# An FFN up-projection loop on one core: each product tied behind the one ahead of it on TensorE

## The chip, the core and the metric

The kernel runs on one core of one Trainium2 chip. The core has engines with queues of their own: TensorE (PE, matrix products, with its weight loads shown as PEld), VectorE (DVE), ScalarE (ACT), GpSimd (POOL) and SyncE (SP, which issues most DMAs). The metric is the device time of one execution in microseconds. A profile of one execution is shown beside it.

## The reference, cut to what matters

A trunk of two layers over a stream x of 1024 positions and 1024 channels, float32. Each layer has a mixer (layer 0 recurrent, layer 1 with attention) and then the gated MLP below. The change touches the product `x @ w_up` of that MLP, in both layers.

```python
D_MODEL, SEQ, DEPTH, D_FF, FFN_CONV = 1024, 1024, 2, 2816, 3

def conv_glu_ffn(x, w_up, conv_w, conv_b, w_down):
    h = causal_depthwise_conv(x @ w_up, conv_w, conv_b)
    gate, val = jnp.split(h, 2, axis=-1)
    return (jax.nn.silu(gate) * val) @ w_down
...
        h = h + conv_glu_ffn(rmsnorm(h, ffn_norm[layer]), ffn_up[layer], ffn_conv_w[layer],
                             ffn_conv_b[layer], ffn_down[layer])
```

## The kernel before

**Precision.** Every float32 product is done as three matmuls. An operand a is split into a high part (a cast on ScalarE, `split`, L389) and a low part (the difference on VectorE, L390); the products are high x high, high x low and low x high. A pair of weight buffers is called wh and wl (or wh2x and wl2x, when it comes from a second pool), the pair of a half-size block dh and dl.

**Blocks.** The up-projection makes 22 blocks of 128 gate channels g and 128 value channels v, numbered f. Positions come in two halves of 512. For f from 1 on, g and v of a block are taken together as a 2 x 2 problem (two outputs, two halves of the input channels), and by a scheme of the Strassen kind it takes seven products instead of eight. Their names in the code are "11", "21", "2", "1", "3", "22", "4". Each product is four chunks of 128 input channels times three matmuls, twelve matmuls of 128 x 512 (`prod`, L777). The input side is made ready once per layer (tiles AH, AL, TH, TL), the weight side per block by `prep_a` to `prep_d`: these sum and split the raw weights (wst) on VectorE and ScalarE for the next block.

**PSUM.** In blocks 2 to 21 four products ("11", "2", "3", "4") accumulate into one bank X, one behind the other, and ScalarE copies X out after each of the first three (p1, L1125; u2, L1135; u3, L1150) and after the fourth (v, L1165). "21" writes y_, the first half of a tile YZ of two banks; "1" and then "22" write z_, its second half. VectorE adds y_ and p1 into one half of g (L1131); ScalarE copies z_ after "1" (p5, L1145); VectorE makes the other halves of v (L1157) and g (L1159). There are four buffers of the kind of X and two of YZ.

**The block before.** While block f is multiplied, the tail of block f-1 runs on the other engines: two activations that start the convolution (L793, L794, `ident`), four taps on VectorE (L799), a silu (L807), a product (L813) and sums that are stored for the down-projection (L823 to L844). In the source the tail's pieces stand between the products of block f. The tail of block 0 stands whole before the loop, behind block 1's products (`prev.whole()`).

**Order.** The program is traced line by line, and a planner then places each instruction on its engine's queue by its own estimate of when the operands are there; among those that are ready, the one traced earlier goes first. Each engine works through its queue in that order and waits at an instruction whose semaphores are not there. `tc.issue_after(ins)` puts what is traced inside it behind `ins` on the same engine, in the planner's order alone, with no semaphore. In the kernel before, the loop holds one such tie for products:

```python
            with tc.issue_after(p4.ins) if f == 2 else nullcontext():
                prod(X, w["a"], 0, "11")
```

p4 is the last matmul of block 1's "4". All other products of the loop are placed as the planner sees fit.

Of the kernel before, what the change touches and what calls it, by code (L numbers as in the profile page):

```python
# [175 lines left out]
def trunk(ctx: ExitStack, tc: tile.TileContext, x, mix0_norm, mix0_w_in, lru_conv_w, lru_conv_b,  # L176
# [74 lines left out]
    def t4(name):  # L251
        return tmp.tile([P, T], F32, tag="t4", bufs=4, name=name)

    def t2(name):
        return tmp.tile([P, H], F32, tag="t2", bufs=4, name=name)

    def pbig(name):
        return psum["big"].tile([P, T], F32, tag="big", name=name)
# [16 lines left out]
    def psml(name):  # L275
        return sml.tile([P, H], F32, tag="sml", name=name)
# [159 lines left out]
    last = {}  # L436

    class Start:
# [24 lines left out]
        def do(self, eng, ins):  # L463

            def trace(fn):
                with ExitStack() as behind:
                    if eng in last:
                        behind.enter_context(tc.issue_after(last[eng].ins))
                    last[eng] = fn()
                return last[eng]  # L470

            return trace(ins)
# [237 lines left out]
    def ffn(ly, norms):  # L710
# [27 lines left out]
        def prep_a(f):  # L738
            w = ws[f] = {"g": W.take(f"{ly}g{f}"), "v": W.take(f"{ly}v{f}"), "a": W.pair()}
            split(*w["a"], w["g"])  # L740

        def prep_s(f, n):
            w = ws[f]
            g, v = w["g"], w["v"]
            if n == 0:
                s1 = w["s1"] = (t2(f"s1{ly}{f}") if w2[0] is None else
                                w2[0].tile([P, H], F32, tag="s1", bufs=2, name=f"s1{ly}{f}")
                                ).rearrange("p (k m) -> p k m", k=4)
                dve.tensor_tensor(s1, v[:, 0:4], v[:, 4:8], op=ALU.add)
                dve.tensor_tensor(v[:, 0:4], g[:, 0:4], v[:, 0:4], op=ALU.subtract)  # L750
            else:
                dve.tensor_tensor(g[:, 0:4], w["s1"], g[:, 0:4], op=ALU.subtract)
                dve.tensor_tensor(g[:, 4:8], g[:, 4:8], g[:, 0:4], op=ALU.subtract)

        def prep_b(f):
            w = ws[f]
            w["b"] = W.pair()
            low = split(*w["b"], w["g"])[1]
            W.done()
            return low  # L760

        def prep_c(f):
            w = ws[f]
            w["c"] = W.pair()
            split(*w["c"], w["v"])
            W.done()

        def prep_d(f):
            w = ws[f]
            w["d"] = [fd.tile([P, 4, P], F32R, tag=t, name=f"{t}{ly}{f}") for t in ("dh", "dl")]  # L770
            split(*w["d"], w["s1"])

        def prod(ps, x, k0, y, first=True):
            (xh, xl), (yh, yl) = x, Y[y]
            for k in range(4):
                for i, (a, b) in enumerate(((xh, yh), (xh, yl), (xl, yh))):
                    last = pe.matmul(ps, a[:, k0 + k], b[:, k],  # L777
                                     start=(first and k == 0 and i == 0),
                                     stop=(k == 3 and i == 2), skip_group_check=True)
            return last  # L780
# [135 lines left out]
        def bring(g, y, j):  # L916

            ks = slice(2 * j, 2 * j + 2)
            r = t4(f"br{ly}{g}{y}{j}").rearrange("p (k t) -> p k t", k=2)
            nc.sync.dma_start(r, hids[ly][g][:, OPS[y], ks])  # L920
            return lambda: split(*(t[:, ks] for t in B[y]), r)

        def brings(g, ys):
            return [lambda y=y, j=j: bring(g, y, j) for y in ys for j in range(2)]
# [137 lines left out]
        def prep(n):  # L1062

            q, i = steps_[n]
            q.preps[i]()
            nxt = quads.index(q) + 1
            if nxt < len(quads):
                if q.form == "A":
                    loads = {1: (0,), 2: (1,)}.get(i, ())
                else:  # L1070
                    loads = {0: (0,), 2: (1,)}.get(i, ())
                for j in loads:
                    quads[nxt].load(j)
# [3 lines left out]
        w = ws[1]  # L1077
        X, R, y_, z_ = (psml(f"{n}{ly}1") for n in ("X", "R", "y", "z"))
# [24 lines left out]
        p4 = prod(X, w["c"], 4, "4", False)  # L1103
# [5 lines left out]
        prev.ident()  # L1109

        first_ = brings(0, ("11", "2", "3", "4"))
        for f in range(2, NF):
            if f == NF - 1:
                W.more = None
                quads[0].load(0)
                came = [b() for b in first_[:2]]
            w, nxt = ws.pop(f), f + 1 if f + 1 < NF else None
            X = psml(f"X{ly}{f}")
            YZ = pbig(f"YZ{ly}{f}")
            y_, z_ = YZ[:, HALF[0]], YZ[:, HALF[1]]  # L1120
            g, v = t4(f"g{ly}{f}"), t4(f"v{ly}{f}")
            with tc.issue_after(p4.ins) if f == 2 else nullcontext():
                prod(X, w["a"], 0, "11")
            p1 = t2(f"p1{ly}{f}")
            act.copy(p1, X)  # L1125
            if nxt:
                prep_a(nxt)
            prev.conv_g()
            prod(y_, w["a"], 4, "21")
            prev.silu()  # L1130
            dve.tensor_tensor(g[:, HALF[0]], y_, p1, op=ALU.add)  # L1131
            prev.conv_v(1)
            prod(X, w["b"], 0, "2", False)
            u2 = t2(f"u2{ly}{f}")
            u2_ = act.copy(u2, X)  # L1135
            if not nxt:
                with tc.issue_after(u2_.ins):
                    for do in came:
                        do()
                came = [b() for b in first_[2:4]]  # L1140
            prev.conv_v(0)
            prev.end()
            prod(z_, w["d"], 0, "1")
            p5 = t2(f"p5{ly}{f}")
            act.copy(p5, z_)  # L1145
            if nxt:
                prep_s(nxt, 0)
            prod(X, w["c"], 0, "3", False)
            u3 = t2(f"u3{ly}{f}")
            u3_ = act.copy(u3, X)  # L1150
            if nxt:
                prep_s(nxt, 1)
                prep_d(nxt)
            else:
                quads[0].load(1)
            prev.sums()
            dve.tensor_tensor(v[:, HALF[1]], p5, u3, op=ALU.add)  # L1157
            prod(z_, w["b"], 4, "22", False)
            dve.tensor_tensor(g[:, HALF[1]], z_, u2, op=ALU.add)  # L1159
            if nxt:  # L1160
                prep_b(nxt)
            else:
                prep(0)
            prod(X, w["c"], 4, "4", False)
            act.copy(v[:, HALF[0]], X)  # L1165
            if nxt:
                prep_c(nxt)
            prev = Tail(f, g, v)
            prev.ident()
# [181 lines left out]
        for f0, n in PLAIN[ly]:  # L1351
            a = slots[f0 - PLAIN[ly][0][0]:][:n]
# [583 lines left out]
    for s_ in order[:-1]:  # L1936
        if s_ == "mix0":
            norm = mix0(norm)
        elif s_ == "mix1":
            norm = mix1(norm)  # L1940
        else:
            norm = ffn(int(s_[-1]), norm)
# [35 lines left out]
```

## Time and profile before

| what | value |
|---|---|
| runs | 2123.05, 2125.86 and 4249.69 us; median 2125.86 |
| profiled execution | 2124.15 us, span 2122.4 us, granted TensorE clock 0.999 |
| TensorE busy | 2089.6 us, 98% of the span, 9580 matmuls |
| VectorE, ScalarE busy | 1603.5 us (76%), 1063.7 us (50%) |
| up-projection loop, f = 2 to 21 | layer 0 from 383.5 to 771.9 us, layer 1 from 1497.8 to 1886.8 us of the span |

Times in the rows are microseconds from the span's start. A row of the timeline gives the start, the duration, engine, line of the kernel, operation, what is written and read by the names of the program, shape and count, and in brackets how long the engine sat idle before and what ended that. A row of the stage table gives a window, its length, and per engine the busy time in it with the number of instructions that touch it; then the granted clock of TensorE as a share, the busy share of the DMA engines and GB/s. Matmuls overlap, and their ends in the record are modelled, so distances between starts are used for TensorE, not durations.

### The profile page before, as it was taken

To read this page: it belongs to the slowest core of one execution; us is meant where nothing else is said; L and a number is where in the kernel's file an instruction comes from. 1 tells how busy PE (TensorE), PEld (TensorE's weight loads), DVE (VectorE), ACT (ScalarE), POOL (GpSimd) and SP (SyncE) were. 2 spreads that over 40 slices of the span, in tenths; PEclk is the share of its full clock that TensorE was granted. 3 is DMA by queue.
4 is the path that set the end of the run, shared out by engine and by line. 5 is a ranking of instruction groups with operands and counts; after the bars stand their busy time and mean duration, and the time that the engine had idled before them with its cause. 6 is when DMAs were issued, how large, how long until landed. Compare 5 with 4: busy or idle time off the path is not lost. (4 is left out here: it accounts for less than half of the span.)

```text
span 2122.4 us, 25660 instructions
## 1 busy us (share of the span) xinstructions
PE 2089.6 (98%) x9580; PEld 1711.9 (81%) x9580; DVE 1603.5 (76%) x2285; ACT 1063.7 (50%) x1478; POOL 76.1 (4%) x122
## 2 busy tenths in 40 slices
PE   8999999999999999999999999999999999999998
PEld 7888888788888878888688888788788888878887
DVE  6755667998888777866576666778998888777865
ACT  5433534655545555333556575654655545555323
POOL 0000000000000000000211111000000000000000
PEclk9999999999999999999999999999999999999999
DMA  6211342233332267761222211452233332267732
GB/s 216 60 50 42 126 151 90 94 120 105 105 109 95 71 233 251 237 180 50 75 68 56 73 56 51 136 183 89 95 119 105 101 112 95 80 234 245 242 102 80
DMA packets 265237, 253.63 MB, mean 120 GB/s; under 512 B 10368, under 2 KB 213952, under 8 KB 265112
## 3 DMA queue, kind: packets, MB, share of 16 engines
q1 hardware_dynamic: 264776, 251.50, 36.8%
q8 instruction: 75, 1.23, 0.2%
q14 instruction: 50, 0.41, 0.1%
q0 software_dynamic: 192, 0.30, 0.1%
q10 hardware_dynamic: 144, 0.20, 0.0%
HBM read 181.40 MB, written 68.45 MB: 118 GB/s over the span
## 5 line engine op out<-in xcount | busy, mean ns | idle before, releaser
L130 ACT CAST wh<-wst 128x1024 fp32r<-128x1024 f32 (+1 forms) x84 | 83.1, 989 | 192.6 <-PE op L396 40.6
L130 DVE TENSOR_TENSOR wl<-wst,wh 128x1024 fp32r<-128x1024 f32 (+1 forms) x84 | 96.3, 1147 | 87.9 <-ACT wh L130 87.8
L777 PE MATMUL X<-TH,wh 128*128 128x512 f32 x384 | 150.4, 392 | 2.1 <-ACT u L1135 1.3
L777 PE MATMUL X<-TH,wl 128*128 128x512 f32 x384 | 149.7, 390 | 0.8 <-DVE wl L390 0.8
L777 PE MATMUL X<-TL,wh 128*128 128x512 f32 x384 | 149.4, 389 | 0.0
L389 ACT CAST wh<-wst 128x1024 fp32r<-128x1024 f32 x96 | 100.2, 1050 | 73.3 <-PE YZ L777 49.6
L390 DVE TENSOR_TENSOR wl<-wst,wh 128x1024 fp32r<-128x1024 f32 x96 | 116.8, 1222 | 11.7 <-ACT wh L389 11.7
L799 DVE SCALAR_TENSOR_TENSOR cg<-g,par_c,cg 128x1023 f32<-128x1023 f32 x88 | 113.0, 1284 | 7.4 <-ACT cg L793 6.2
L799 DVE SCALAR_TENSOR_TENSOR cv<-v,par_c,cv 128x1023 f32<-128x1023 f32 (+1 forms) x88 | 112.7, 1281 | 0.0
L777 PE MATMUL YZ<-AH,wh 128*128 128x512 f32 x240 | 93.5, 389 | 0.0
L777 PE MATMUL YZ<-AL,wh 128*128 128x512 f32 x240 | 93.4, 389 | 0.0
L777 PE MATMUL YZ<-AH,wl 128*128 128x512 f32 x240 | 93.4, 389 | 0.0
L1135 ACT COPY u<-X 128x512 f32<-128x512 f32 x40 | 23.5, 587 | 138.7 <-PE X L777 138.7
L777 PEld LDWEIGHTS X<-TH,wh 128*128 128x128 f32 x384 | 72.1, 188 | 20.1 <-ACT u L1135 2.6
L777 PEld LDWEIGHTS X<-TH,wl 128*128 128x128 f32 x384 | 72.1, 188 | 16.7 <-DVE wl L390 1.6
L777 PEld LDWEIGHTS X<-TL,wh 128*128 128x128 f32 x384 | 72.1, 188 | 14.7
L396 PE MATMUL op<-AH,wh 128*128 128x512 f32 x192 | 75.6, 395 | 0.0
L396 PE MATMUL op<-AL,wh 128*128 128x512 f32 x192 | 74.7, 390 | 0.7 <-DVE AL L390 0.7
L396 PE MATMUL op<-AH,wl 128*128 128x512 f32 x192 | 74.6, 389 | 0.0
L1157 DVE TENSOR_TENSOR v<-p,u 128x512 f32<-128x512 f32 x40 | 27.7, 692 | 59.6 <-ACT u L1150 59.6
L793 ACT ACTIVATE cg<-g,par_c 128x1024 f32<-128x1024 f32 x44 | 54.8, 1246 | 30.0 <-DVE g L1159 25.5
L1687 ACT ACTIVATE P<-P,sm 128x128 f32<-128x128 f32 (+3 forms) x64 | 49.7, 777 | 30.4 <-DVE sm L1684 30.0
(798 smaller groups left out, 6286.7 us busy)
## 6 DMA issues: line engine op xcount, KB each, us to landing
wst<-in_ffn_up_dram SPq DMA_DIRECT2D x88, 512.0 KB
br<-hids SPq DMA_DIRECT2D x56, 512.0 KB
wst<-in_mix_w_in_dram SPq DMA_DIRECT2D x40, 512.0 KB
wst<-in_mix_w_out_dram SPq DMA_DIRECT2D x32, 512.0 KB
hids<-cv SPq DMA_DIRECT2D x32, 512.0 KB
hT_o<-hdr SPq DMA_DIRECT2D x32, 256.0 KB
hdr<-hT_o SPq DMA_DIRECT2D x32, 256.0 KB
hids<-t SPq DMA_DIRECT2D x32, 256.0 KB
```

Source lines behind the costliest of these rows:

```text
L130: did = self.nc.scalar.copy(wh[:, :k, :m], w[:, :k, :m]), self.eng.tensor_tensor(wl[:, :k, :m], w[:, :k, :m], wh[:, :k, :m].bitcast(F32), ...
L389: return (act.copy(h, src), (eng or dve).tensor_tensor(l, src, h.bitcast(F32), op=ALU.subtract))
L390: (eng or dve).tensor_tensor(l, src, h.bitcast(F32), op=ALU.subtract))
L396: last_mm = pe.matmul(ps, a[:, k], b[:, k, s], start=(k == 0 and i == 0), stop=(k == DC - 1 and i == 2))
L777: last = pe.matmul(ps, a[:, k0 + k], b[:, k], start=(first and k == 0 and i == 0), stop=(k == 3 and i == 2), skip_group_check=True)
L793: act.activation(self.cg, self.g, AF.Identity, scale=taps[2](f), bias=bias(f))
L799: dve.scalar_tensor_tensor(dst[:, dl:], src[:, :T - dl], taps[j](c), dst[:, dl:], op0=ALU.mult, op1=ALU.add)
L1135: u2_ = act.copy(u2, X)
L1157: dve.tensor_tensor(v[:, HALF[1]], p5, u3, op=ALU.add)
L1687: act.activation(Pt[:, :n], Pt[:, :n], AF.Exp, bias=low, scale=-1.0, accum_out=sm[:, 6:7])
```

## The change

Inside the loop every product goes through a helper that ties it behind the last matmul of the product before it, beginning with block 1's "4". The order of the products on TensorE is then that of the source: "11", "21", "2", "1", "3", "22", "4", block after block, for f from 2 on. Nothing else is edited; the single tie for f = 2 is taken over by the helper.

```diff
         first_ = brings(0, ("11", "2", "3", "4"))
+        last["p"] = p4
+
+        def prod_(*a):
+
+            with tc.issue_after(last["p"].ins):
+                last["p"] = prod(*a)
+
         for f in range(2, NF):
...
-            with tc.issue_after(p4.ins) if f == 2 else nullcontext():
-                prod(X, w["a"], 0, "11")
+            prod_(X, w["a"], 0, "11")
...
-            prod(y_, w["a"], 4, "21")
+            prod_(y_, w["a"], 4, "21")
...
-            prod(X, w["b"], 0, "2", False)
+            prod_(X, w["b"], 0, "2", False)
...
-            prod(z_, w["d"], 0, "1")
+            prod_(z_, w["d"], 0, "1")
...
-            prod(X, w["c"], 0, "3", False)
+            prod_(X, w["c"], 0, "3", False)
...
-            prod(z_, w["b"], 4, "22", False)
+            prod_(z_, w["b"], 4, "22", False)
...
-            prod(X, w["c"], 4, "4", False)
+            prod_(X, w["c"], 4, "4", False)
```

## The prediction

> **What bounds the kernel now.** I read the page first, then the stage table over the two up-projection loops, then TensorE's and VectorE's timelines at the head of the loop.
>
> ```profile
> span 2122.4 us, 25660 instructions
> ...
> PE 2089.6 (98%) x9580; PEld 1711.9 (81%) x9580; DVE 1603.5 (76%) x2285; ACT 1063.7 (50%) x1478; POOL 76.1 (4%) x122
> ```
>
> TensorE is idle for 32.8 us of the whole span, so an edit that only orders its work can win little. Where in the changed stage does it lose time? The stage table (PE busy time and count first) takes two blocks and a half at the head of each layer's loop, and an equal stretch right behind:
>
> ```profile
> core 0: us, PE busy (x) PEld busy (x) DVE busy (x) ACT busy (x) POOL busy (x), PEclk, DMA share, GB/s
> 383.48:430.59 47.11, 45.05 (x194) 35.50 (x192) 46.61 (x55) 29.42 (x35) 0.00 (x0) 1.00 0.33 107
> 446.91:494.02 47.11, 47.11 (x209) 39.05 (x208) 41.19 (x47) 24.68 (x31) 0.00 (x0) 1.00 0.33 104
> 1497.81:1544.96 47.15, 45.08 (x193) 35.50 (x192) 46.64 (x55) 29.41 (x35) 0.00 (x0) 1.00 0.33 106
> 1561.28:1608.43 47.15, 47.15 (x209) 38.97 (x208) 40.93 (x46) 24.57 (x31) 0.00 (x0) 1.00 0.33 104
> ```
>
> At the head some 15 matmuls fewer fit into the same time, and VectorE is busy 46.61 of 47.11 us. Behind it TensorE never idles, and VectorE has slack (41.19). Both layers do the same to 0.04 us.
>
> What is the order today? The stage table for matmuls into YZ alone: "21", "1" and "22" write YZ, the other four products write X, so the source's order X Y X Z X Z X must show as an alternation, 2.72 us each. First inside block 5, then inside blocks 2 and 3:
>
> ```profile
> 447.40:449.60 2.20, 0.00 (x0) 1.00 0.84 244
> 450.10:452.30 2.20, 2.20 (x11) 1.00 0.11 33
> 452.80:455.00 2.20, 0.00 (x0) 1.00 0.03 7
> 455.50:457.70 2.20, 2.20 (x11) 1.00 0.27 103
> 458.20:460.50 2.30, 0.00 (x0) 1.00 0.30 114
> 461.00:463.20 2.20, 2.20 (x11) 1.00 0.35 95
> ...
> 392.60:395.60 3.00, 0.00 (x0) 1.00 0.41 122
> 396.90:399.20 2.30, 0.00 (x0) 1.00 0.46 129
> 399.30:400.90 1.60, 0.61 (x2) 1.00 0.00 0
> 401.40:403.70 2.30, 2.30 (x11) 1.00 0.30 114
> ```
>
> Block 5 is in the source's order already, and so is everything up to block 21 of either layer. Only blocks 2 and 3 and the first product of block 4 are not: in block 2, "2" (to 395.6) is followed by "3" (396.42 to 399.2), then by seven early matmuls of block 3, and only at 401.00 by "1". The change therefore acts on about 47 us of each layer.
>
> **The change part by part.** It adds no instruction, no DMA and no semaphore: each product's twelve matmuls get an edge behind the last matmul of the product ahead. SyncE's and GpSimd's queues are not passed by anything. What moves is which matmul TensorE waits at.
>
> *Price of a matmul and of the four waits of today.* TensorE's timeline, one row each where something starts or waits (columns: start, duration, operation, count, idle before it and what ended that):
>
> ```profile
> 383.48 0.39 PE L777 MATMUL YZ<-AH,wh 128*128 128x512 f32 x1
> ...
> 384.32 0.49 PE L777 MATMUL X<-TH,wh 128*128 128x512 f32 x1 [0.22 <-ACT u L1096]
> ...
> 387.18 0.39 PE L777 MATMUL X<-AH,wh 128*128 128x512 f32 x1
> ...
> 389.90 0.39 PE L777 MATMUL YZ<-AH,wl 128*128 128x512 f32 x1
> ...
> 393.14 0.50 PE L777 MATMUL X<-TH,wl 128*128 128x512 f32 x1 [0.36 <-DVE wl L390]
> ...
> 396.42 0.50 PE L777 MATMUL X<-TH,wh 128*128 128x512 f32 x1 [0.67 <-ACT u L1135]
> ...
> 401.00 0.39 PE L777 MATMUL YZ<-AH,dh 128*128 128x512 f32 x1
> ...
> 414.52 0.50 PE L777 MATMUL X<-AH,wh 128*128 128x512 f32 x1 [0.79 <-ACT wh L389]
> ...
> 430.59 0.39 PE L777 MATMUL YZ<-AH,wh 128*128 128x512 f32 x1
> ```
>
> The product from 387.18 to 389.90 gives 2.72 us for twelve, 0.2267 us each; a matmul after a wait takes 0.50 instead of 0.39, so a restart costs 0.11. From 383.48 to the start of block 4's "21" at 430.59 run 192 matmuls (one product of block 1, fourteen of blocks 2 and 3, one of block 4): 43.52 us of work in 47.11, so **3.59 us** are lost today.
>
> *The same 192 in the source's order.* (i) Block 1's "4" waits for the copy u3 until 384.32 as now; the two matmuls of block 2's "21" that fill a part of that wait are pushed behind it. Lost: 0.84, and 0.11 for the restart. (ii) "11" of block 2 runs from 387.18 to 389.90, all twelve of "21" to 392.62. (iii) "2" starts at 392.62, since p1's copy is done:
>
> ```profile
> 390.10 0.59 ACT L1125 COPY p<-X 128x512 f32<-128x512 f32 x1 [0.54 <-PE X L777]
> ```
>
> Its third matmul needs wl, which lands as now for 393.14 instead of the 393.07 at which TensorE would be there. Lost: 0.07 and 0.11. "2" has issued at 395.52. (iv) Now comes "1", and here is the price. VectorE's timeline:
>
> ```profile
> 390.67 1.29 DVE L799 SCALAR_TENSOR_TENSOR cv<-v,par_c,cv 128x1023 f32<-128x1023 f32 x1
> 391.86 2.37 DVE L390 TENSOR_TENSOR wl<-wst,wh 128x1024 fp32r<-128x1024 f32 x2
> 394.13 1.29 DVE L799 SCALAR_TENSOR_TENSOR cg<-g,par_c,cg 128x1023 f32<-128x1023 f32 x1
> ...
> 398.90 1.23 DVE L390 TENSOR_TENSOR wl2x<-wst,wh2x 128x1024 fp32r<-128x1024 f32 x1
> 400.04 0.70 DVE L1131 TENSOR_TENSOR g<-YZ,p 128x512 f32<-128x512 f32 x1
> ...
> 645.50 0.69 DVE L1131 TENSOR_TENSOR g<-YZ,p 128x512 f32<-128x512 f32 x1
> ```
>
> "1" writes the other half of YZ, yet it waits for the addition L1131 that reads the first half. A later block shows that wait openly: L1131 ends at 646.19 there, and "1" starts 0.05 us behind it.
>
> ```profile
> 646.24 0.50 PE L777 MATMUL YZ<-AH,dh 128*128 128x512 f32 x1 [0.15 <-DVE g L1131]
> ```
>
> In block 2 L1131 runs from 400.04 to 400.74, behind block 0's four taps (394.13 to about 399.0) and the low half of block 3's weights, all of which stand earlier in the source, so I leave it there. "1" can start at 400.80: a stall of 400.80 - 395.52 = 5.28 us, plus 0.11. Today "3" and seven matmuls of block 3 hide it. Queued behind "1" on TensorE is everything else of the loop; on ScalarE the copies p5 and u3 follow later, VectorE has its own backlog and loses nothing.
> (v) After that nothing is late. "1" issues until 403.63, "3" until 406.35, "22" until 409.07 (p5's copy takes 0.59 us like p1's and is done by 404.7), "4" until 411.79 (u3 done by about 407.3), block 3's "11" and "21" until 417.2. The cast wh that ends for 414.52 today is done before TensorE gets to a product that needs it, so that wait of 0.79 us goes. L1131 of block 3 can start at 417.5 and "1" needs it by 419.95: two operations of VectorE fit ahead. The buffers of the split weights come free some 2 us later, and so do the products that ask for the next ones.
> Also, matmuls right behind a restart come 0.233 apart instead of 0.2267 for a while; today that is 3.59 less the waits and restarts, about 0.25. I take 0.2.
>
> New loss: 0.95 + 0.18 + 5.39 + 0.2 = 6.72 against 3.59: **+3.1 us a layer**, 6.3 for both. From there to the end TensorE is 98% busy and gives nothing back.
>
> *The clock behind a stall of 5.3 us.* No row of before shows TensorE waiting that long inside the loop, but two places show what the granted clock does:
>
> ```profile
> 1351.80:1355.20 3.40, 2.41 (x11) 1.73 (x12) 3.13 (x10) 3.36 (x6) 1.04 (x2) 0.97 0.75 224
> 1355.20:1358.60 3.40, 3.40 (x13) 2.83 (x14) 3.29 (x12) 3.34 (x10) 0.41 (x1) 0.53 0.89 285
> ...
> 2115.64 0.28 PE L1288 MATMUL f<-TL,AH 128*128 128x256 f32 x1
> ...
> 2118.80:2122.40 3.60, 0.00 (x0) 0.00 (x0) 0.00 (x0) 0.00 (x0) 0.00 (x0) 0.61 0.39 146
> ```
>
> In the attention stage about a microsecond of idling out of 3.4 was followed by 3.4 us at 0.53 of the clock; over the last 3.6 us the share is 0.61 on average, that is one half for the last 2.8, from 2119.6 on, 3.7 us after the last matmul ended (2115.92). So a stall of 5.28 us probably ends with the clock at one half. Bounds: nothing, and two such stretches, 2 x 3.4 x 0.47 = 3.2 us a layer. I take one, the row at 1355.20: 3.4 x 0.47 = **1.6 us a layer**, 3.2 for both.
>
> [...]
>
> **Sum.** The profiled execution took 2124.15 us (the span 2122.4 and 1.75 around it), between the runs' lowest of 2123.05 and their median of 2125.86. 2124.15 + 6.3 + 3.2 = **2133.7 us**, 0.4% slower than the median. A measurement here tells about 2% from no change, so this is "no change".
>
> **The rivals.**
> *The clock holds.* For it: a wait of 2.24 us at the kernel's start, and the stretch around it at full clock:
>
> ```profile
> 35.35 1.10 PE L484 MATMUL rb<-diag,one 128*128 128x512 f32 x2 [2.24 <-DVE diag L478]
> ...
> 30.00:40.00 10.00, 7.76 (x37) 5.99 (x36) 4.67 (x10) 3.04 (x6) 0.00 (x0) 1.00 1.00 366
> ```
>
> Against it: the two places above. 2124.15 + 6.3 = 2130.5.
> *VectorE takes L1131 early.* If the planner, seeing TensorE held by "1", puts L1131 ahead of block 0's taps, it ends by about 395, the stall is gone, and the source's order loses 0.95 + 0.18 + 0.2 = 1.3 instead of 3.6: 2124.15 - 4.6 = 2119.6. Against it: the taps stand earlier in the source, and in the trace L1131 came behind all of them although "21" had finished at about 392.5.
> *The change does nothing, or half of it.* L1131 moves ahead of some of the taps, and the stall shrinks to what is lost today: about 2124.2. For it: 17 of 20 blocks a layer keep their order anyway.
> *Slower, in the later blocks.* A new plan could put one more tap ahead of L1131 in each block; since "1" may not be passed any more by anything, it is TensorE that waits. Price: at most 1.29 less the overlap of 0.10 to the next (390.67 to 391.86), 1.19 us, in 36 blocks: 43 us, 2177 with the head's loss. At 646.24 there is no cover for it at all; where L1131 is done well ahead of "1" less remains, about half: 2155. It passes 2% only if nearly all 36 blocks pay the whole 1.18. Against it: the later blocks are in the source's order on TensorE already, and wait 0.15 us there.
>
> **How the numbers follow.** Forecast 54%, clock holds 25%, L1131 early 8%, nothing 7%, later blocks 6%, half of that above 2%. The range leaves out L1131 early and the later blocks, 14%. Its low end is "nothing" with the lowest run shown (about 2122); its high end the forecast with two half-rate stretches a layer (+3.2), one more operation ahead of L1131 in each layer (+2.4) and the median's distance from the profiled execution (+1.7): 2141, rounded to 2142. Faster by over 2%: 1%, for a plan I have not seen; slower by over 2%: 3%; within: 96%.
>
> **What would show it.** In the changed profile the YZ rows must alternate from block 2 on; "1" of block 2 must start right behind L1131 with 5 us of idling, in both layers; "3" must follow it, and the waits behind u L1135 and wh L389 must be gone; the clock must be below 1.00 right behind the stall; the later blocks must look as now. I am wrong if L1131 stands elsewhere in VectorE's order, if "1" turns out to wait for something else, or if the later blocks or the attention stage come out in another order.

## The result, and the profile after

| kernel | median | runs | ratio to before, 95% interval |
|---|---|---|---|
| before | 2125.59 us (four of 2123.05 to 2125.86, one of 4249.69) | 5 | |
| after | 2136.07 us (2134.66 to 2136.39) | 5 | 1.0051 [1.0040, 1.0062] |

One run of before, of 4249.69 us, took twice the time of the others, and the ratio leaves it out. The change makes the kernel slower by half a per cent. The profiled execution of after took 2136.39 us, 12.2 more than that of before. From the page:

```profile
span 2134.7 us, 25670 instructions
...
PE 2094.0 (98%) x9580; PEld 1717.0 (80%) x9580; DVE 1604.1 (75%) x2285; ACT 1064.6 (50%) x1478; POOL 75.6 (4%) x122
```

The counts are those of before, and the busy share is still 98%: at this level nothing shows. The waits of TensorE, longest first, name the new one at once (a row gives who waited for whom, the sum in us, how often, and the longest). It stands alone at the top, two times 5.1 us; in the list of before it was the last, with 0.2 us in all:

```profile
PE YZ L777 <- DVE g L1137: 10.2, 2, 5.1
PE S L1676 <- DVE sm L1690: 3.5, 5, 1.0
PE rb L484 <- DVE diag L478: 2.8, 2, 2.2
```

(L1137 is the addition that was L1131: the helper has moved the lines by six.) In the stage table for matmuls into YZ, the head of layer 0's loop now shows the source's order: "2", nothing for 5.2 us, then "1", "3", "22", "4". The third column from the right is the granted clock:

```profile
394.40:396.90 2.50, 0.08 (x1) 1.00 0.34 99
397.20:402.40 5.20, 0.00 (x0) 0.82 0.47 136
402.60:407.20 4.60, 4.60 (x11) 0.50 0.33 118
408.10:410.30 2.20, 0.00 (x0) 1.00 0.00 0
410.80:413.00 2.20, 2.20 (x11) 1.00 0.42 160
413.50:415.70 2.20, 0.00 (x0) 1.00 0.58 218
```

TensorE's timeline at the same place. "2" starts its last matmul at 397.05, "1" its first at 402.53; then the matmuls come 0.43 us apart instead of 0.23:

```profile
397.05 0.39 PE L777 MATMUL X<-TH,wl 128*128 128x512 f32 x1
402.53 0.79 PE L777 MATMUL YZ<-AH,dh 128*128 128x512 f32 x1 [5.09 <-DVE g L1137]
403.12 0.63 PE L777 MATMUL YZ<-AL,dh 128*128 128x512 f32 x1
403.55 0.63 PE L777 MATMUL YZ<-AH,dl 128*128 128x512 f32 x1
...
407.39 0.40 PE L777 MATMUL YZ<-AH,dl 128*128 128x512 f32 x1
407.63 0.39 PE L777 MATMUL X<-TH,wh 128*128 128x512 f32 x1
```

And VectorE's, with what it does in the meantime:

```profile
395.88 1.27 DVE L799 SCALAR_TENSOR_TENSOR cg<-g,par_c,cg 128x1023 f32<-128x1023 f32 x1
397.07 1.27 DVE L799 SCALAR_TENSOR_TENSOR cv<-v,par_c,cv 128x1023 f32<-128x1023 f32 x1
398.27 1.28 DVE L799 SCALAR_TENSOR_TENSOR cg<-g,par_c,cg 128x1022 f32<-128x1022 f32 x1
399.46 1.28 DVE L799 SCALAR_TENSOR_TENSOR cv<-v,par_c,cv 128x1022 f32<-128x1022 f32 x1
400.65 1.22 DVE L390 TENSOR_TENSOR wl2x<-wst,wh2x 128x1024 fp32r<-128x1024 f32 x1
401.79 0.68 DVE L1137 TENSOR_TENSOR g<-YZ,p 128x512 f32<-128x512 f32 x1
```

The stage table, first over the head of the loop before, then over the same stretch after (both start behind the same matmul) and an undisturbed one further on, and last the half-rate stretch of each layer:

```profile
383.48:433.30 49.82, 47.76 (x205) 37.75 (x204) 49.32 (x58) 31.49 (x37) 0.00 (x0) 1.00 0.35 114
385.18:435.00 49.82, 44.06 (x182) 35.53 (x182) 47.77 (x56) 28.55 (x34) 0.00 (x0) 0.93 0.35 111
453.90:503.70 49.80, 49.80 (x220) 40.87 (x219) 42.95 (x49) 26.92 (x34) 0.00 (x0) 1.00 0.30 98
400.60:407.40 6.80, 4.87 (x12) 3.81 (x13) 6.80 (x9) 2.69 (x3) 0.00 (x0) 0.50 0.22 80
1520.20:1526.90 6.70, 3.88 (x9) 3.11 (x10) 6.70 (x7) 3.56 (x3) 0.00 (x0) 0.50 0.14 52
```

In the same 49.82 us 182 matmuls now touch the window instead of 205, and the mean clock in it is 0.93.

**Where the 12.2 us are.** I measure each loop from the first matmul of block 1 to the last one of block 21. Layer 0 took 404.48 us before and 409.55 after, layer 1 405.14 and 409.47: 5.07 + 4.33 = **9.4 us in the two loops**. The other 2.8 us lie where nothing was edited: 1.7 ahead of the first loop and 1.1 between the two, and in each of these places lies a stretch at half clock that this execution had and the profiled one of before had not:

```profile
35.30:38.80 3.50, 3.49 (x6) 2.10 (x7) 1.42 (x3) 0.62 (x2) 0.00 (x0) 0.51 1.05 409
786.20:789.70 3.50, 3.25 (x8) 2.58 (x9) 3.50 (x4) 3.50 (x6) 0.00 (x0) 0.51 0.72 208
```

The first lies ahead of the change, where both programs are the same instruction for instruction. Such stretches come and go between executions, and the times of one kernel spread by several microseconds (33 runs of before on one chip: 2123.67 to 2131.1, with mean clocks of 0.997 to 0.999). For differences of 2 us I therefore go by the loops of the profiled executions as well as by medians.

### The profile page after: what moved, and what is told of

It reads as the page before. It is cut to its first block, busy times and chain, and to the rows that moved or that the text cites. A ratio compares the mean times of both kernels' runs of the same rounds, so it can differ in the third digit from the quotient of the medians.

```text
span 2134.7 us, 25670 instructions
## 1 busy us (share of the span) xinstructions
PE 2094.0 (98%) x9580; PEld 1717.0 (80%) x9580; DVE 1604.1 (75%) x2285; ACT 1064.6 (50%) x1478; POOL 75.6 (4%) x122
## 5 line engine op out<-in xcount | busy, mean ns | idle before, releaser
L777 PE MATMUL YZ<-AH,dh 128*128 128x512 f32 x160 | 65.0, 407 | 10.6 <-DVE g L1137 10.2
```

The lines of the kernel that those rows point to most:

```text
L777: last = pe.matmul(ps, a[:, k0 + k], b[:, k], start=(first and k == 0 and i == 0), stop=(k == 3 and i == 2), skip_group_check=True)
```

## The experiments

Two theories after the first result. **A**: the tie of block 2's "1" carries the loss, because "1" waits for the addition and nothing may pass it. **B**: VectorE is behind at the head of each loop, and this is the bound; the addition is only the place where it shows, and the free order of before is what covered it.

| kernel | median (runs) | ratio, 95% interval | loops, layer 0 and 1 |
|---|---|---|---|
| before | 2126.11 (25), 2126.84 (33) | | 404.48, 405.14 |
| one product untied | 2131.69 (10) | 1.0022 [1.0012, 1.0031] | 407.07, 407.70 |
| own banks, tied | 2129.7 (10) | 1.0015 [1.0005, 1.0025] | 405.95, 406.93 |
| own banks, free | 2127.73 (10) | 1.0006 [0.9997, 1.0016] | 404.38, 404.87 |
| stall filled, tied | 2136.77 (4) | 1.0051 [1.0036, 1.0066] | 411.17, 410.50 |
| taps left out, tied | 2124.54 (10) | 0.9988 [0.9979, 0.9997] | 404.91, 406.29 |
| taps left out, free | 2126.24 (10) | 0.9997 [0.9986, 1.0007] | 405.53, 404.23 |
| GpSimd, own banks, tied | 2128.22 (10) | 1.0008 [0.9999, 1.0017] | 405.76, 406.74 |
| GpSimd, own banks, free | 2129.16 (11) | 1.0007 [0.9998, 1.0015] | 404.35, 408.12 |

The last column is of one profiled execution each, and a fall of the clock of 3.41 us, which costs some 1.6 us where TensorE is busy (an estimate: 3.41 x 0.47, from the 0.53 of the row at 1355.20 in before), can lie in it by chance. One lies in layer 1 of "own banks, tied" and of "GpSimd, own banks, free", in layer 0 of "taps left out, free", and in both layers of "GpSimd, own banks, tied"; the other four kernels of the table and before have none in the loops.

**One product untied.** In both layers, only block 2's "1" is left to the planner:

```diff
-            prod_(z_, w["d"], 0, "1")
+            (prod if f == 2 else prod_)(z_, w["d"], 0, "1")
```

> Theory A (the one tie of block 2's "1" carries the loss, because "1" waits for VectorE's L1131-addition and nothing may pass it): with that product alone untied, "3" runs in the stall. Lost at the head of a layer: 0.95 (u3) + 0.18 (wl) + 1.0 ("3" waits for u2's copy) + 1.7 (rest of the stall, under 2 us, so the clock holds) + 0.2 = 4.0 us against 3.6 of before: about 2125 us, 11 us faster than the changed kernel. Rival (the ties of the other products cost too, since block 3 may no longer fill in): 2130 us or more.

Measured: 5.2 us over before in the loops, so that one tie makes 4.2 of the 9.4 us (by the medians 4.9 of 10.5). The planner put "1" behind "3", and its wait shrank as foreseen, with the granted clock at 1.00 (layer 0, from 383.5 to 440 us). But a second wait opened that I had not counted: "22" now follows "1" directly and waits for the copy p5.

```profile
400.76 0.50 PE L777 MATMUL YZ<-AH,dh 128*128 128x512 f32 x1 [1.39 <-DVE g L1137]
404.47 0.50 PE L777 MATMUL YZ<-AH,wh 128*128 128x512 f32 x1 [0.68 <-ACT p L1151]
```

The median is past the rival's 2130: theory A is right on a large piece and wrong as the whole. Of the 5.2 us, 3.4 lie in blocks 1 to 3, where the other ties keep block 3 from filling these gaps, as the rival has it; the other 1.8 lie in later blocks, and why is not shown.

**Own banks.** The two halves of YZ become two tiles, so that "1" and the addition no longer touch the same one; once on the changed kernel, once on the kernel before. (Both come out of the pool of two that YZ had, so a block now takes both buffers of it.)

```diff
-            YZ = pbig(f"YZ{ly}{f}")
-            y_, z_ = YZ[:, HALF[0]], YZ[:, HALF[1]]
+            y_, z_ = (pbig(f"{n}{ly}{f}")[:, HALF[0]] for n in "YZ")
```

> All products tied, but the two halves of YZ are tiles of their own, so that "1" need not wait for the addition that reads the first. Theory A: the stall ahead of block 2's "1" is gone, the clock holds there, and 1.3 us a layer are lost instead of 3.6: 2119.6 us, faster than both kernels. Rival B (VectorE's backlog is the bound, the addition only the place where it shows): the stall turns up in front of block 3's "2", whose low weights come at 413 to 414 on the old clock while TensorE would ask at 409: 4 to 5 us a layer, with or without a fall of the clock 2128 to 2133 us.

> The same two tiles without the ties. Theory A: "1" of block 2 is placed before "3" by the planner, and the waits of before shrink: 2120 to 2122 us. Rival B: TensorE's early matmuls go on filling VectorE's backlog, nothing changes: 2124 us.

In the tied kernel "1" starts 0.23 us behind the last matmul of "2", five microseconds ahead of the addition, which ran at 402.22:

```profile
396.92 0.40 PE L777 MATMUL X<-TH,wl 128*128 128x512 f32 x1
397.15 0.39 PE L777 MATMUL Z<-AH,dh 128*128 128x512 f32 x1
```

So the wait belonged to the shared tile. Yet the kernel is not faster than before, as theory A had it, but 3.3 us slower in the loops. TensorE's waits in layer 0's loop name the new places, and the longest is the one that B had named, the low half of block 3's weights:

```profile
PE X L777 <- DVE wl L390: 1.7, 1, 1.7
PE Z L777 <- ACT p L1150: 1.2, 1, 1.2
PE X L777 <- ACT p L1130: 0.7, 1, 0.7
PE X L777 <- ACT u L1096: 0.7, 1, 0.7
```

B's price for it was too high (1.7 and 1.9 us instead of 4 to 5), and its total of 2128 to 2133 held with the help of other losses: the wait for p5 and a fall of the clock in layer 1. Without ties the planner did place "1" ahead of "3", as A had it, and block 2 then lost nothing. But block 3 lost more, in layer 0 2.0 us on the cast wh, which itself waited 2.6 us for VectorE, and the time did not change (interval across 1), as B expected and A did not.

**The stall filled.** Twenty matmuls of no use ahead of block 2's "1", in a bank of their own:

```diff
+            if f == 2:
+                wm = psml(f"wm{ly}")
+                for _ in range(20):
+                    with tc.issue_after(last["p"].ins):
+                        last["p"] = pe.matmul(wm, w["b"][0][:, 0], Y["2"][0][:, 0], ...)
             prod_(z_, w["d"], 0, "1")
```

> The changed kernel with twenty matmuls of no use (4.5 us) ahead of block 2's "1" in each layer, in a bank of their own. They fill the stall and take nothing else. If the clock falls because TensorE idles there, it now holds: the twelve matmuls of "1" come 0.23 apart instead of 0.43, 2.4 us a layer, 2136.1 - 4.9 = 2131.2 us. If the half-rate stretch has another cause: 2136.

```profile
402.60:409.40 6.80, 6.80 (x30) 5.63 (x31) 6.38 (x7) 3.61 (x6) 0.00 (x0) 1.00 0.21 77
1521.50:1528.30 6.80, 6.80 (x30) 5.64 (x31) 6.80 (x8) 3.52 (x5) 0.00 (x0) 1.00 0.22 80
```

The clock held: in 6.8 us TensorE now touches 30 matmuls, where the changed kernel touched 12. So here the idling brought the clock down: 0.50 over these 6.8 us in the changed kernel, 1.00 with the stall filled. The time did not follow, 2136.8 against 2131.2 expected. "1" starts at 402.52 and the addition runs at 401.79, as in the changed kernel, and "1" is then done 2.3 us earlier. TensorE reaches the later blocks that much earlier relative to VectorE, and waits there, which the changed kernel did not do:

```profile
498.96 0.50 PE L777 MATMUL YZ<-AH,dh 128*128 128x512 f32 x1 [0.94 <-DVE g L1137]
```

Summed over layer 0's blocks behind the head, such losses are 4.0 us here and 0.9 in the changed kernel. Whether VectorE is late there because it had 2.3 us less to catch up, or because of another order, stays open. Its queue is indeed in another order than in the changed kernel from 410 us on: in block 3, for one, the addition stands behind one tap of the block before (420.10) and not behind three (422.27).

**Taps left out.** Block 0's four convolution taps are left out of the computation, with the ties and without:

```diff
             def tap(self, dst, src, c, j):
+                if self.f == 0:
+                    return
```

> The changed kernel without block 0's four convolution taps (left out of the computation, some 4.8 us of VectorE's work ahead of block 2's addition in each layer). Theory B (VectorE's backlog at the head makes the stall, the order of source only exposes it): the addition ends by 397, "1" waits about 1 us instead of 5.1, the clock holds; lost about 2.4 us a layer instead of 7.7 with the clock: 2136 - 10.6 = 2125, and within 3 us of the same kernel without ties. Rival C (the order itself costs, whatever VectorE has to do, because nothing may fill in): at least 5 us above the kernel without ties.

> The kernel before without the same four taps. Theory B: the waits at the head shrink from 3.6 us a layer towards 1.5, 2126 - 4 = 2122. Rival (TensorE was covered already): 2126.

This pair decides between B and C. Between A and B it does not, since an addition that comes in time leaves no wait in A either; for that, "own banks" is the test. With some 4.8 us less for VectorE at the head, the addition stands at 396.94, and "1" follows its predecessor without a gap:

```profile
398.73 0.39 PE L777 MATMUL X<-TH,wl 128*128 128x512 f32 x1
398.96 0.39 PE L777 MATMUL YZ<-AH,dh 128*128 128x512 f32 x1
```

The tied kernel comes to 2124.5 us (0.9988 of before, where the changed one had 1.0051), and the free one with the same omission to 2126.2. With the backlog that much smaller the source's order costs nothing that these medians can tell, and the rival by which the order itself costs 5 us is out. A smaller cost is not: by the loops of the profiled executions the tied kernel takes 1.4 us more than the free one, and 3.0 if the free one's fall of the clock is taken off. The only wait left at the tied kernel's head behind u3's is one of 1.4 us on p1's copy. That the free kernel gained nothing was not expected: most of its waits at the head went, but p1's copy was late instead, and in that execution the clock fell behind it (the loop of layer 0 has a 3.41 us stretch at one half from 395.6).

**GpSimd.** Own banks, and two low halves of weights at the head go to GpSimd, which idles there; tied and free:

```diff
-            split(*w["a"], w["g"])
+            split(*w["a"], w["g"], pool if f == 3 else None)
...
-            split(*w["c"], w["v"])
+            split(*w["c"], w["v"], pool if f == 2 else None)
```

> All tied, YZ as two tiles, and two of VectorE's low halves at the head (block 2's third pair, block 3's first, 1.2 us each) on GpSimd, which is idle there and took 1.3 to 1.8 us for half the size. Theory B: the 1.7 to 1.9 us wait for block 3's low weights goes, 2129.7 - 4 = 2126, level with before. Rival (GpSimd is too slow, or slows VectorE down): 2130 or more.

> The same two moves to GpSimd and the two tiles, without ties. Theory B: the 2.1 and 1.3 us waits ahead of block 3's "2" go: 2127.7 - 3.5 = 2124, some 2 us faster than before. Rival (as above): 2127 or more.

Neither beats before: measured were 2128.2 us tied, between B's 2126 and the rival's 2130, and 2129.2 free, in the rival's range. In the tied kernel the wait for block 3's low weights is gone, but p5's copy is late by 2.0 us. It stands on ScalarE behind the silu (1.06 us) and its table load (1.28 us), and these behind a cast that waited 2.9 us for the DMA of the raw weights. Nor was VectorE relieved. A tap that meets GpSimd's work takes 3.4 us instead of 1.27 and ends about one tap's length behind it:

```profile
392.03 2.69 POOL L390 TENSOR_TENSOR wl<-wst,wh 128x1024 fp32r<-128x1024 f32 x1 [65.51 <-ACT wh L389]
392.39 3.41 DVE L799 SCALAR_TENSOR_TENSOR cg<-g,par_c,cg 128x1023 f32<-128x1023 f32 x1
395.72 1.27 DVE L799 SCALAR_TENSOR_TENSOR cv<-v,par_c,cv 128x1023 f32<-128x1023 f32 x1
```

It is so in all eight places of the two kernels (3.27 to 3.43 us), so each move cost VectorE 2.0 to 2.2 us to save the 1.22 of a low half: the second part of the rival, that GpSimd slows VectorE down. In the free kernel TensorE waits for GpSimd itself, which took 2.36 us for what VectorE does in 1.22:

```profile
404.20 0.50 PE L777 MATMUL X<-AH,wl2x 128*128 128x512 f32 x1 [1.76 <-POOL wl2x L390]
```

Taking one wait away at the head hands it to the next operand; no version here beats the kernel before by more than these runs can tell, apart from "taps left out, tied", which leaves work out.

## Why the prediction was right, and where its terms were off

The forecast was no change beyond 2%, 2133.7 us and in the range; measured were 2136.07.

*The order of today and the place* held: from block 5 on nothing moved on TensorE, and the loss lies in 47 us at each head. *The waits of today go* held: of those of before, the one on u3 is left (0.68 at 386.02 instead of 0.22, as in step (i)), and the low weights' wait of step (iii) is too short to be listed.

*Step (iv), the stall*: forecast 5.28 us, measured 5.25 between where the first matmul of "1" would have come and where it came, in both layers. The addition stayed behind the four taps and the low half of block 3's weights, in the same order. The rival in which it moves ahead is out, and so is the one in which the later blocks pay. (In block 3 the addition did move behind two more taps, to 422.27, but "1" came only at 423.98, so nothing waited.)

*Step (v), nothing is late behind it* held until block 7 of layer 0, where 0.2 us are lost.

*The clock* is the term that was mis-sized. I took one stretch of 3.4 us, 1.6 us a layer. It was a double one, 6.83 us, which began 2.0 us before the stall ended in layer 0; the other 4.9 us took "1" from 2.72 us to 5.1. In layer 1 it began 2.9 us before the end, and "1" took 4.7. With the restart's 0.11 taken off, which the forecast has in step (iv), the price was 2.3 us and 1.9, inside the bounds of 0 and 3.2. What I had not reckoned with is that the end of the stall, at 402.53 and 1523.02, still fell into the first 3.41 us at half rate, and that another 3.41 us at half rate followed in both layers (rows in the last section). Of the 0.2 us for slow spacing behind a restart less than 0.1 a layer came on top.

*The sum*: 9.5 us forecast for the two loops, 9.4 measured. That they agree so well is partly luck: the clock cost 0.9 us more in all than I took, some 0.3 of the 0.4 us for slow spacing were not there, and the later blocks lost 0.6 us less than before. What the forecast left out are the half-rate stretches elsewhere, 2.8 us in the profiled execution; they explain the distance from 2133.7 to 2136.

*The reason* needs one addition. I had called the wait for the addition the price and VectorE's backlog its cause. The experiments bear out that it takes both. Taking away the wait alone brings the two loops from 9.4 to 3.3 us above before, some 1.6 of them (an estimate, 3.41 x 0.47) by a fall of the clock; shortening the backlog, with wait and order left as they are, brings them to 1.6 above before. The addition is what the prediction left out: with the wait gone TensorE is not faster than before, because the backlog then shows at other operands.

The clock did not fall at the end of the stall but inside it: at 400.6 TensorE had idled for 3.1 us and at 1520.1 for 2.2. And in layer 1 of "own banks, tied" a wait of 1.9 us came ahead of a fall:

```profile
1534.60:1538.00 3.40, 3.40 (x9) 2.66 (x9) 3.40 (x4) 1.24 (x1) 0.00 (x0) 0.51 0.66 188
```

## What to carry to other kernels

An order that is free for the planner is worth most where another engine is behind: look at that engine's busy share at the head of a stage (here 46.6 of 47.1 us) before tying work on the one that is nearly full. Find the first product whose operand comes from the late engine, and subtract: the difference of two rows gave the stall to 0.03 us. And price a stall twice, once for the wait and once for the clock behind it: at the two of 5.1 us it fell to 0.50 both times, behind nine waits of 1.75 to 2.04 us in the loops five times. Before work goes to an idle engine, look at whether the busy one keeps its pace beside it (here a tap on VectorE took 3.4 us beside GpSimd instead of 1.27).

## What the runs showed of the hardware that I had not expected

The half-rate stretches of these traces last 3.41 or 6.83 us, and one came behind a wait of a length at which I had the clock hold in my expectation for "one product untied": 1.9 us, in the run above. In the attention stage about a microsecond of idling came ahead of one. Whether a given short wait brings one differs between executions. The wait of 2.24 us at the start, ahead of any edit, is in both traces, and the 3.41 us up to its end hold 1.18 us of matmuls in before and 1.17 in after. Full clock follows in before:

```profile
31.94:35.35 3.41, 1.18 (x10) 0.87 (x9) 1.18 (x4) 1.18 (x3) 0.00 (x0) 1.00 1.06 405
35.35:38.76 3.41, 3.41 (x13) 2.52 (x14) 2.25 (x4) 1.24 (x2) 0.00 (x0) 1.00 1.04 402
```

and 0.50 in after:

```profile
31.93:35.34 3.41, 1.17 (x11) 0.87 (x9) 1.18 (x4) 1.18 (x3) 0.00 (x0) 1.00 1.07 404
35.34:38.75 3.41, 3.41 (x6) 2.06 (x7) 1.39 (x2) 0.61 (x1) 0.00 (x0) 0.50 1.05 407
```

What sets the two apart was not tested. Here are the 3.41 us just ahead of a fall in the loops, in after (layers 0 and 1) and in "own banks, tied" (layer 1), and as the last row a stretch of the same length in layer 0 of "own banks, tied" that holds a wait of 1.75 us and has no fall behind it:

```profile
397.16:400.57 3.41, 0.28 (x2) 0.00 (x0) 3.41 (x3) 2.49 (x3) 0.00 (x0) 1.00 0.73 211
1516.73:1520.14 3.41, 1.20 (x6) 0.66 (x4) 3.41 (x4) 1.61 (x2) 0.00 (x0) 1.00 1.00 287
1531.13:1534.54 3.41, 1.51 (x8) 0.94 (x7) 3.41 (x6) 3.29 (x4) 0.00 (x0) 1.00 0.84 315
414.97:418.38 3.41, 1.67 (x8) 1.06 (x7) 3.41 (x5) 2.99 (x4) 0.00 (x0) 1.00 0.57 215
```

In the attention stage of before a fall came behind 3.4 us with 2.41 us of matmuls, so no limit can be read from these rows. The two long stretches of after, each in two parts of 3.41 us, first layer 0, then layer 1:

```profile
400.57:403.98 3.41, 1.45 (x4) 1.16 (x5) 3.41 (x5) 1.82 (x3) 0.00 (x0) 0.50 0.03 5
403.98:407.39 3.41, 3.41 (x10) 2.64 (x8) 3.41 (x5) 0.90 (x1) 0.00 (x0) 0.50 0.41 154
1520.14:1523.55 3.41, 0.53 (x1) 0.50 (x2) 3.41 (x4) 2.36 (x3) 0.00 (x0) 0.50 0.04 13
1523.55:1526.96 3.41, 3.41 (x9) 2.64 (x8) 3.41 (x4) 1.24 (x1) 0.00 (x0) 0.50 0.27 99
```

The stall's end lies in the first part, of which TensorE was busy for 1.45 and 0.53 us, and the clock stayed at one half for the second, which TensorE filled. The short stretch of after at 35.34 was filled at once (3.41 us) and ended after 3.41 us.

The stretches go with the spread of the times: of the ten runs of "own banks, free", the one with a mean clock of 0.999 took 2123.53 us, the five with 0.996 took 2127.72 to 2130.17.
